# A batch-norm matmul: row-wise spread by small copies, one block turned behind the last product, one fused scale and shift

## The chip, the cores and the metric

The kernel runs on one core of a Trainium2 chip. The metric is the device time of one execution in microseconds (us); the time shown for a kernel is the median of its runs. Five engines work side by side, each in the order of its own queue: PE (TensorE, matrix products), DVE (VectorE), ACT (ScalarE), POOL (GpSimd) and SP (SyncE, which here only issues transfers). Transfers are carried out by 16 DMA engines that all queues share.

## The reference

```python
def reference(x, weight, gamma, beta, eps):      # x: 16 x 512 x 1024, weight: 1024 x 768
    y = np.matmul(x, weight)
    mean = np.mean(y, axis=(0, 1), keepdims=True)
    var = np.var(y, axis=(0, 1), keepdims=True)
    y_norm = (y - mean) / np.sqrt(var + eps)
    return (gamma * y_norm + beta).astype(np.float32)
```

x has 8192 rows of 1024 numbers, the output 8192 rows of 768 channels, all float32. Every channel is normalized over all 8192 rows, so that no output of a channel can be written before all of that channel's products are done.

## The kernel before

**Tiling.** The rows are cut into 16 chunks c of 512, the channels into 6 tiles nt of 128, counted from 0. x is loaded as bf16 and transposed by DVE into `xT_sb`. All of x and all products stay in the core's memory, the products as bf16 in `y_sb`.

**Tiles 0 and 1** are computed with the rows on the partitions. Their mean and square sums pass through `sum1`, `sum2` and `sum3`, which are free afterwards. When the statistics are known, `spread` (L894, a float32 product with the identity `ident32`) lays scale and shift out along a row in a PSUM bank, DVE multiplies (L930), POOL or DVE adds (L935), and SP stores.

**Tiles 2 to 5** are computed with the channels on the partitions, one unit `col_unit` of 8 products of 128x512 per chunk (L568). DVE takes statistics (L704), ACT copies the products out of PSUM (L708). `finish_tasks` combines the statistics into scale and shift. Then blocks of two chunks (1024 rows) are normalized in place (L1016 on ACT for tile 2, L1019 on DVE for tiles 3 and 4) and must be turned back, since the output has the rows outermost. `col_block` does it in one of two ways, by `MODE`:
- "xact": SP issues a DMA transpose (L1190), ACT converts the result to float32 (L1202), SP stores (L1172).
- "pe": PE makes 8 transposes of 128x128 (L1037) into a PSUM bank, ACT copies the bank to float32 (L1180), SP stores. The transposes are hosted: `mm` puts one of them behind each product of a later unit.

**Raw blocks.** The blocks at chunks 0 and 2 of tiles 2 and 4 are turned by a DMA transpose before they are normalized (L1099), at about 100 us. Their scale and shift then lie along the row as for tiles 0 and 1: `raw_spread` (L1119) makes two float32 products into a bank (L896), and ACT copies the shift half to `sum2` (L1130). `raw_block` multiplies on DVE out of the bank (L1144), adds on POOL out of `sum2` (L1148) and stores (L1152).

**Copies of x.** `xT_sb` of most chunks interleaves pairs of contraction rows, so that a product reads it with a stride of two. For the chunks in `PARTED` ACT makes a contiguous copy `x_pl` early on; for those in `LATE`, `part_chunk` has POOL or DVE make it (four copies of 128x1024 for a chunk, L540) for the units of tiles 4 and 5. The chunks in `SINGLE` are transposed without the interleave.

**The end.** The last chunk of tile 5 is multiplied in two halves (`last_unit`, L746). Then, one after the other: DVE's statistics of the last half (L753), `aggregate` (L1254), `root` on ACT (L1257), `affine` on DVE (L1264 to L1266), the first `norm_part` (L1289), PE's transposes (L1037), ACT's copy (L1302) and SP's store (L1305), for 11 pieces of 256 to 1024 rows.

**What sets the order.** Each step is a `task` with a due time, its engines, its dependences and a cost written by hand. `arrange` (L122) plays these through once and emits the instructions of every engine in the order that results; a list of 8 PSUM banks, slots of the ring buffer for outgoing blocks and the like take part. At run time each queue is in order: an instruction that waits holds up all behind it.

Of the kernel before, what the change touches and what calls it, by code (L numbers as in the profile page):

```python
# [227 lines left out]
def kernel(  # L228
# [9 lines left out]
    nc = tc.nc  # L238
# [28 lines left out]
    GY = 2  # L267
    PAD = 54
    HELD = 0
    ASTAT = {2:tuple(range(4,16))}  # L270
    RC = C - 2
    XT, YB, SQ = C - EARLY, 28, 3
    ADDED = (0,6,16,28,40)
    PARTED, LATE, SINGLE = (4,5,7,8,9,10), (12,13,14,15,11), (2,3,6)
    MODE = {2:'xact',3:'xact',4:('pe',)*2+('xact',)*1+('pe',)*5}
    MODE = {nt: m if isinstance(m, tuple) else (m,) * (C // GY) for nt, m in MODE.items()}
# [62 lines left out]
    rstd = singles.tile([P, 1], f32)  # L339
    warm = singles.tile([P, 1], f32)  # L340

    seq(nc.scalar.activation(warm, eps_sb, AF.Sqrt))
# [9 lines left out]
    def task(prio, engines, emit, deps=(), lock=False, **kw):  # L352
        t = Task(prio, engines, emit, deps, **kw)
        t.lock = lock
        tasks.append(t)
        return t
# [10 lines left out]
    def pe(occ):  # L367
        return {"PE": (occ, occ + 0.03)}
# [72 lines left out]
    for kind, n, *n1 in order:  # L441
# [12 lines left out]
        if m0 == M // 2:  # L454
            affine = task(t, {"SP": (5.0, 7.0)}, load_affine, [x_ready[m0 // CH - 3, 0, JW]])
        slot = Slot(rings, rows // 32 * KQ // 2)
# [662 lines left out]
    def raw_spread(nt, fin_task):  # L1119
        bank = Slot(banks)  # L1120
        at = (0, NA, 2 * NA)[nt - GA] // 2

        def emit(eng):
            a_ps = psum.tile([P, CH], f32, tag="b")
            bank.tile = a_ps
            spread(a_ps[:, 0:P], scale, nt)
            spread(a_ps[:, P:2 * P], shift, nt)

        def keep(eng):
            seq(nc.scalar.copy(sum2[:, at:at + P], bank.tile[:, P:2 * P]))  # L1130

        t = task(clock[0] + 1.0, pe(0.45), emit, [fin_task], takes=[bank])
        k = task(clock[0] + 1.0, act(0.25), keep, [t], uses=[bank])
        raw_aff[nt] = bank, t, k, sum2[:, at:at + P]

# [25 lines left out]
    def col_block(nt, c, due, fin_task, held=False):  # L1161
# [46 lines left out]
        return b  # L1208

    held = []  # L1210
    STEP = {2: 1.9, 3: 2.3, 4: 2.3}
# [47 lines left out]
    def first_term(eng):  # L1259
        seq(nc.vector.scalar_tensor_tensor(  # L1260
            tmp[:, one], mv[:, nt, 0:1], -1.0, gamma_sb[:, one], op0=ALU.mult, op1=ALU.mult))

    def affine(eng):
        seq(nc.vector.reciprocal(rstd, std[:, one]))  # L1264
        seq(nc.vector.tensor_mul(scale[:, one], rstd, gamma_sb[:, one]))
        seq(nc.vector.scalar_tensor_tensor(  # L1266
            shift[:, one], tmp[:, one], rstd, beta_sb[:, one], op0=ALU.mult, op1=ALU.add))

# [4 lines left out]
    ft = task(E - 50.0, dve(0.1), first_term, [ag])  # L1273
    af = task(E - 50.0, dve(0.45), affine, [ro, ft])
    for i, (hn, hc, hf) in enumerate(held):
        b = col_block(hn, hc, E + 0.3 + 0.3 * i, hf)
        b.deps.append(col_end[nt, C - 1, len(PIECES) - 1][0])
    ends = [(0, 0, QR), (0, QR, QR), (1, 0, CH), (2, 0, CH)] + [(c, 0, 2 * CH) for c in range(3, C - 1, 2)]
    ends += [(C - 1, 0, CH)]
    for c, r0, rows in ends:  # L1280
# [5 lines left out]
        for i in range(n):  # L1286
            def norm_part(eng, c=c + i, r0=r0, rows=min(rows, CH)):
                part = y(nt, c)[:, r0:r0 + rows]
                seq(nc.vector.tensor_scalar(  # L1289
                    part, part, scale[:, one], shift[:, one], op0=ALU.mult, op1=ALU.add))  # L1290

            norms.append(task(due + 0.6 * i, dve(0.323 if rows >= CH else 0.26), norm_part, [af] + keeps,
                              uses=[y_of(nt, c + i)]))
# [59 lines left out]
```

## Time and profile before

| what | value |
|---|---|
| median of 3 runs | 207.62 us (207.26 to 207.69) |
| profiled execution, device time | 207.92 us |
| its span, first to last instruction | 206.0 us |
| mean granted clock of TensorE in the span | 0.981 |
| busy: PE, DVE, ACT, POOL | 191.4, 157.6, 139.5, 129.4 us |
| read from and written to memory | 36.71 MB and 25.17 MB |
| DMA transposes L1190, L1099 | 15 and 4 |

The profiled execution took 207.92 us, of which 1.92 us lie around its span; it is 0.30 us above the median of the runs. Up to about 100 us the kernel loads x and multiplies tiles 0 and 1, and parts of the others, as x comes in; from there to 188.4 us PE multiplies tiles 2 to 5 while the outputs of the earlier tiles are normalized, turned and stored. From 188.4 us tile 5's statistics are closed and its 4.2 MB are normalized, turned and stored. A busy time counts an instruction from its start to its end, also where the next one overlaps it; the granted clock is the share of TensorE's full clock that its throttle gave it, and the DMA share is the mean over the 16 DMA engines.

### The profile page before, as it was taken

The page shows a single profiled execution, that of the slowest core. Times are in us where ns is not written, and L with a number is a line of the kernel's source. Part 1 is how long each engine was busy: PE and PEld are TensorE (multiplying, and loading weights), DVE is VectorE, ACT ScalarE, POOL GpSimd, SP SyncE. Part 2 cuts the span into 40 slices and gives each one's busy share as a digit, 9 for nine tenths or more (in the row PEclk, how much of TensorE's full clock was granted, in tenths as well). Part 3 has the DMA queues.
Part 4 walks back from the last instruction along what each step waited for, and adds up shares of the span by engine and source line. Part 5 has one row for each costly group of instructions (what it writes and reads, how often), then busy time and mean ns, then how long its engine had stood idle before and what let it go on. Part 6 is the DMA issues. An engine that isn't in the chain of part 4 may idle for free.

```text
span 206.0 us, 3500 instructions
## 1 busy us (share of the span) xinstructions
PE 191.4 (93%) x1218; PEld 117.8 (57%) x1218; DVE 157.6 (76%) x239; ACT 139.5 (68%) x248; POOL 129.4 (63%) x143
## 2 busy tenths in 40 slices
PE   7979999999999999999999999999999999996910
PEld 3457564747488888777875444444444445553900
DVE  4022879999999999969989998888999648947900
ACT  2000561369979999998979767996575877875960
POOL 7676964887499989997304998599955440440000
PEclk9999999999999999999999999999999999999695
DMA  4999999999999999999665898899999999999898
GB/s 76 143 199 196 174 196 196 196 198 196 190 193 197 197 196 197 196 197 195 109 153 179 311 339 300 253 349 278 294 325 233 322 312 296 338 344 346 250 347 254
DMA packets 98561, 48.73 MB, mean 237 GB/s; under 512 B 24304, under 2 KB 98032, under 8 KB 98544
## 3 DMA queue, kind: packets, MB, share of 16 engines
q0 software_dynamic: 34624, 18.36, 64.9%
q1 hardware_dynamic: 63920, 30.16, 52.9%
q8 instruction: 9, 0.15, 0.3%
q14 instruction: 8, 0.07, 0.1%
HBM read 36.71 MB, written 25.17 MB: 300 GB/s over the span
## 4 chain that ended last, share of the span: by engine, by line
PE 86%; DMA 3%; ACT 3%; POOL 3%; issue 1%; DVE 1%; ACTq 0%; POOLq 0%
PE y_ps L568 53%; PE y_ps L503 24%; PE y_ps L807 4%; DMA ring<-in_x_dram 3%; ACT o_sb L1302 3%; PE o_ps L1037 2%; POOL ring L399 1%; POOL w_sb L383 1%; PE a_ps L896 1%; PE y_ps L746 1%; PE o_ps L1067 0%; ACTq L1348 0%; PE idle_ps L584 0%; PE tot_ps L864 0%; DVE fin L753 0%
## 5 line engine op out<-in xcount | busy, mean ns | idle before, releaser
L568 PEld LDWEIGHTS <-w_sb 128*128 128x128 bf16 x520 | 50.4, 97 | 56.9
L568 PE MATMUL y_ps<-x_pl,w_sb 128*128 128x512 bf16 x264 | 61.3, 379 | 0.0
L399 POOL DMA_DIRECT2D ring<-in_x_dram x76 | 47.4, 630 | 14.0 <-DMA ring<-in_x_dram 5.4
L568 PE MATMUL y_ps<-xT_sb,w_sb 128*128 128x512 bf16 (+1 forms) x256 | 55.7, 370 | 0.0
L503 PE MATMUL y_ps<-w_sb,xT_sb 128*128 128x256 bf16 x448 | 50.4, 272 | 1.3 <-DMA ring<-in_x_dram 1.2
L503 PEld LDWEIGHTS <-xT_sb 128*128 128x128 bf16 x448 | 43.7, 98 | 8.6 <-DVE xT_sb L428 1.9
L428 DVE STREAM_TRANSPOSE xT_sb<-ring 128x1024 f32<-128x1024 f32 (+1 forms) x29 | 31.2, 1111 | 14.4 <-DMA ring<-in_x_dram 14.3
L704 DVE BATCH_NORM_STATS2 stats<-y_ps 128x6 f32<-128x512 f32 x46 | 30.6, 686 | 11.2 <-PE y_ps L568 11.0
L708 ACT CAST y_sb<-y_ps 128x512 bf16<-128x512 f32 x51 | 29.2, 591 | 13.8 <-DVE stats L704 11.6
L935 POOL TENSOR_TENSOR ring<-ring,sum 128x1024 f32<-128x1024 f32 (+1 forms) x11 | 23.8, 2186 | 14.6 <-ACT y_ps L717 11.1
L652 ACT ACTIVATE sq_sb<-y_ps 128x512 f32<-128x512 f32 x28 | 16.4, 611 | 18.6 <-PE y_ps L503 18.3
L659 POOL TENSOR_TENSOR sum<-sum,sq_sb 128x512 f32<-128x512 f32 x20 | 25.6, 1280 | 3.8 <-ACT sq_sb L652 2.7
L540 ACT COPY x_pl<-xT_sb 128x1024 bf16<-128x1024 bf16 x24 | 24.4, 1054 | 1.7 <-DVE xT_sb L428 1.7
L655 DVE TENSOR_TENSOR sum<-y_ps,sum 128x512 f32<-128x512 f32 x28 | 18.9, 675 | 6.4 <-ACT sq_sb L652 5.3
L665 ACT CAST y_sb<-y_ps 128x512 bf16<-128x512 f32 x28 | 16.0, 601 | 7.7 <-DVE sum L655 7.4
L540 POOL COPY x_pl<-xT_sb 128x1024 bf16<-128x1024 bf16 x15 | 16.4, 1131 | 7.7 <-DVE x_pl L540 4.9
L1202 ACT CAST ring<-ring 128x1024 f32<-128x1024 bf16 x15 | 15.8, 1050 | 2.5 <-DMA ring<-y_sb 2.3
L930 DVE TENSOR_TENSOR ring<-y_sb,a_ps 128x1024 f32<-128x1024 bf16 (+1 forms) x16 | 16.7, 1079 | 0.7 <-DMA out_dram<-ring 0.7
L1148 POOL TENSOR_TENSOR ring<-ring,sum 128x1024 f32<-128x1024 f32 x4 | 9.7, 2422 | 10.9 <-DVE ring L1144 10.8
L1037 PE MATMUL o_ps<-ident,y_sb 128*128 128x128 bf16 x104 | 14.5, 248 | 2.1 <-DVE y_sb L1289 2.0
L421 DVE STREAM_TRANSPOSE xT_sb<-ring 128x2048 bf16<-128x2048 bf16 x6 | 13.5, 2288 | 0.2 <-DMA ring<-in_x_dram 0.2
L584 PE MATMUL idle_ps<-idle_sb 128*128 128x512 f32 x18 | 10.9, 765 | 1.5 <-DVE idle_sb L315 1.5
(97 smaller groups left out, 154.8 us busy)
## 6 DMA issues: line engine op xcount, KB each, us to landing
out_dram<-ring SPq DMA_DIRECT2D x38, 512.0 KB, 3.8
ring<-in_x_dram POOLq DMA_DIRECT2D x52, 256.0 KB, 8.7
out_dram<-o_sb SPq DMA_DIRECT2D x6, 512.0 KB, 4.4
ring<-in_x_dram POOLq DMA_DIRECT2D x16, 128.0 KB, 6.2
w_sb<-in_weight_dram POOLq DMA_DIRECT2D x8, 192.0 KB, 6.2
out_dram<-ring SPq DMA_DIRECT2D x4, 256.0 KB, 3.1
ring<-in_x_dram POOLq DMA_DIRECT2D x4, 192.0 KB, 7.9
out_dram<-o_sb SPq DMA_DIRECT2D x3, 256.0 KB, 2.5
```

Of the source, the lines that this page charges most:

```text
L399: bi = seq(nc.gpsimd.dma_start(x_bf[32 * i:32 * i + 32], src[:, :, KQ * i:KQ * (i + 1)]))
L428: seq(nc.vector.transpose(dst, src[:, :, jw0:jw1]))
L503: seq(nc.tensor.matmul(y_ps[:, s], x_of(c, jw, e, t * P, (t + 1) * P), w_sb[:, jw, e, 0:NA], start=(s == 0 and jw == 0 and e == 0), stop=( ...
L540: seq(nc.scalar.copy(dst, pairs) if eng == "ACT" else ENG[eng].tensor_copy(dst, pairs))
L568: seq(nc.tensor.matmul(y_ps, w_sb[:, jw, e, nt * P:(nt + 1) * P], moving(c, jw, e, q0 * QR, q1 * QR, parted), start=(jw == 0 and e == 0 an ...
L655: seq(nc.vector.tensor_add(sum1, slot.tile[:, 0:n], sum1))
L659: seq(ENG[eng].tensor_add(acc, acc, state["sq"][:, 0:n]))
L704: seq(nc.vector.bn_stats(dst, slot.tile))
L708: seq(nc.scalar.copy(y(nt, c), slot.tile))
L930: seq(nc.vector.tensor_mul(slot.o, y_row[c].y[:, s0:s1], aff[0][:, None, :].to_broadcast([P, n, NA])))
L935: seq(ENG[eng].tensor_add(slot.o, slot.o, row[:, None, :].to_broadcast([P, n, NA])))
L1037: seq(nc.tensor.transpose(dst, src, ident))
```

## The change

The diff does the following:
- `raw_spread` uses no products any more. DVE copies the scale column and the shift column into two 32-wide fields of `sum1` and transposes them in 32x32 blocks into `sum3` (`turn`). Four copies of 32x2x32 gather the four partition groups into a row on the first 32 partitions of `sum2` (`gather`), and three copies of 32x256 deal this row to the other partition groups (`deal`). Gather and deal may each run on POOL or ACT; in the emitted order both stand on POOL for tile 2, and for tile 4 gather stands on ACT and deal on POOL. ACT then copies the row of 256 into a PSUM bank (`keep`). POOL's add reads the shift half in `sum2` as before, DVE's multiplication the scale half in the bank.
- Chunk 11 leaves `LATE`: its `x_pl` is not made, and the units of tiles 4 and 5 read it from `xT_sb`. Chunk 10, its neighbour, leaves the group of late chunks too, which moves both in the order of tile 3.
- `MODE[4]` is "pe" for all blocks. Before, its third entry (chunks 4 and 5) was "xact"; the first two entries belong to the raw blocks.
- `HELD` is 1: the block of chunks 14 and 15 of tile 4 is given to the new function `held_block`. It is normalized early, its 8 transposes stand on PE behind the last product (two groups of 4 in two banks), ACT copies each group (128x512), and SP stores each (256 KB). The second copy and the copy-out of the very last products (`last_keep`, L756) stand behind `root` on ACT.
- The last scale and shift come from one instruction over two columns: `coef` holds gamma and minus mean times gamma, `base` holds 0 and beta, and `fss = coef * rstd + base`. The constant columns are filled on POOL (`terms`, three small instructions, in its queue behind the merging of the sums at L793).
- `PAD`, the unused columns behind the statistics, goes from 54 to 50; three two-column tensors (`coef`, `base`, `fss`) are new.

In the emitted order of the changed kernel the four float32 products per raw tile are gone from PE, 40 hosted transposes of tile 4 remain (five blocks, as before), the last of them one unit earlier, and 8 stand between the last product and tile 5's own transposes.

```diff
--- before.py
+++ after.py
@@ -265,14 +265,14 @@
     GA = 2
     NA = GA * P
     GY = 2
-    PAD = 54
-    HELD = 0
+    PAD = 50
+    HELD = 1
     ASTAT = {2:tuple(range(4,16))}
     RC = C - 2
     XT, YB, SQ = C - EARLY, 28, 3
     ADDED = (0,6,16,28,40)
-    PARTED, LATE, SINGLE = (4,5,7,8,9,10), (12,13,14,15,11), (2,3,6)
-    MODE = {2:'xact',3:'xact',4:('pe',)*2+('xact',)*1+('pe',)*5}
+    PARTED, LATE, SINGLE = (4,5,7,8,9,10), (12,13,14,15), (2,3,6)
+    MODE = {2:'xact',3:'xact',4:('pe',)*8}
     MODE = {nt: m if isinstance(m, tuple) else (m,) * (C // GY) for nt, m in MODE.items()}
     RAW, RAWADD, RAWDUE = {2:(0,2),4:(0,2)}, {2:'POOL',3:'POOL',4:'POOL'}, {2:14.0,3:8.0,4:8.0}
     RING = 3 * CH // 32 * KQ // 2
@@ -338,6 +338,9 @@
     tmp = singles.tile([P, NT], f32)
     rstd = singles.tile([P, 1], f32)
     warm = singles.tile([P, 1], f32)
+    coef = singles.tile([P, 2], f32)
+    base = singles.tile([P, 2], f32)
+    fss = singles.tile([P, 2], f32)
 
     seq(nc.scalar.activation(warm, eps_sb, AF.Sqrt))
     touched = singles.tile([P, 2, TOUCH], f32)
@@ -452,7 +455,7 @@
         rows = n1[0] if kind == "p" else QR if kind == "x" else CH
         m0 = n if kind == "p" else n * rows
         if m0 == M // 2:
-            affine = task(t, {"SP": (5.0, 7.0)}, load_affine, [x_ready[m0 // CH - 3, 0, JW]])
+            affine_loads = affine = task(t, {"SP": (5.0, 7.0)}, load_affine, [x_ready[m0 // CH - 3, 0, JW]])
         slot = Slot(rings, rows // 32 * KQ // 2)
         between = BETWEEN if m0 == 0 else {}
         also = sum(len(v) for v in between.values())
@@ -1118,20 +1121,41 @@
 
     def raw_spread(nt, fin_task):
         bank = Slot(banks)
-        at = (0, NA, 2 * NA)[nt - GA] // 2
-
-        def emit(eng):
+        k = sorted(RAW).index(nt)
+        row = sum2[:, 2 * P * k:2 * P * (k + 1)].rearrange("p (i n) -> p i n", n=P)
+        wide, turned = sum1[:, NA + 64 * k:NA + 64 * (k + 1)], sum3[:, 64 * k:64 * (k + 1)]
+        both = turned.rearrange("p (i n) -> p i n", n=32)
+        now = clock[0] + RAWDUE[nt] + 2.0
+
+        def quadrant(i):
+            return slice(32 * i, 32 * i + 32)
+
+        def turn(eng):
+            for i, src in enumerate((scale, shift)):
+                seq(nc.vector.tensor_copy(wide[:, quadrant(i)], src[:, nt:nt + 1].to_broadcast([P, 32])))
+            seq(nc.vector.transpose(turned, wide))
+
+        def move(eng, dst, src):
+            seq(nc.scalar.copy(dst, src) if eng == "ACT" else nc.gpsimd.tensor_copy(dst, src))
+
+        def gather(eng):
+            for i in range(4):
+                move(eng, row[0:32, :, quadrant(i)], both[quadrant(i)])
+
+        def deal(eng):
+            for i in range(1, 4):
+                move(eng, row[quadrant(i)], row[0:32])
+
+        def keep(eng):
             a_ps = psum.tile([P, CH], f32, tag="b")
             bank.tile = a_ps
-            spread(a_ps[:, 0:P], scale, nt)
-            spread(a_ps[:, P:2 * P], shift, nt)
-
-        def keep(eng):
-            seq(nc.scalar.copy(sum2[:, at:at + P], bank.tile[:, P:2 * P]))
-
-        t = task(clock[0] + 1.0, pe(0.45), emit, [fin_task], takes=[bank])
-        k = task(clock[0] + 1.0, act(0.25), keep, [t], uses=[bank])
-        raw_aff[nt] = bank, t, k, sum2[:, at:at + P]
+            seq(nc.scalar.copy(a_ps[:, 0:2 * P], row.rearrange("p i n -> p (i n)")))
+
+        d = task(now, dve(0.35), turn, [fin_task], True)
+        g = task(now, {"POOL": (0.8, 0.85), "ACT": (0.9, 1.0)}, gather, [d])
+        s = task(now, {"POOL": (1.2, 1.25), "ACT": (1.0, 1.1)}, deal, [g])
+        t = task(now, act(0.4), keep, [s], takes=[bank])
+        raw_aff[nt] = bank, t, s, row[:, 1]
 
     def raw_block(nt, c, due):
         rslot, turned = raw[nt, c]
@@ -1206,6 +1230,27 @@
             task(due + 1.2, {"SP": (0.38, 0.4)}, store, [d], dma=count * P * P * 4 / 1024 * STORE * 1.024,
                  uses=[slot])
         return b
+
+    def held_block(nt, c, due, fin_task, last_mm, root_task):
+        yslot = y_of(nt, c)
+        keeps = [col_end[nt, c + i][1] for i in range(GY)]
+        count = RT
+        a = task(due - 20.0, dve(0.45), norm(nt, c, GY), [fin_task] + keeps, True, uses=[yslot])
+        for i in range(GY):
+            slot = Slot(rings, count * P)
+            m0 = (c + i) * CH
+            b, bank = turn_block(due - 1.0 + 0.1 * i, nt, m0, count, [a, last_mm], [yslot])
+
+            def copy(eng, slot=slot, bank=bank):
+                slot.o = piece(slot).rearrange("p (s n) -> p s n", n=P)
+                seq(nc.scalar.copy(slot.o, bank.tile))
+
+            def store(eng, slot=slot, m0=m0):
+                seq(nc.sync.dma_start(
+                    out_flat[m0:m0 + count * P, nt * P:(nt + 1) * P].rearrange("(s p) n -> p s n", p=P), slot.o))
+
+            d = task(due - 60.0 + 15.0 * i, act(0.48), copy, [b] + ([root_task] if i else []), takes=[slot], uses=[bank])
+            task(due, {"SP": (0.38, 0.4)}, store, [d], dma=count * P * P * 4 / 1024 * STORE * 1.024, uses=[slot])
 
     held = []
     STEP = {2: 1.9, 3: 2.3, 4: 2.3}
@@ -1258,23 +1303,28 @@
 
     def first_term(eng):
         seq(nc.vector.scalar_tensor_tensor(
-            tmp[:, one], mv[:, nt, 0:1], -1.0, gamma_sb[:, one], op0=ALU.mult, op1=ALU.mult))
+            coef[:, 1:2], mv[:, nt, 0:1], -1.0, gamma_sb[:, one], op0=ALU.mult, op1=ALU.mult))
+
+    def terms(eng):
+        seq(nc.gpsimd.tensor_copy(coef[:, 0:1], gamma_sb[:, one]))
+        seq(nc.gpsimd.memset(base[:, 0:1], 0.0))
+        seq(nc.gpsimd.tensor_copy(base[:, 1:2], beta_sb[:, one]))
 
     def affine(eng):
         seq(nc.vector.reciprocal(rstd, std[:, one]))
-        seq(nc.vector.tensor_mul(scale[:, one], rstd, gamma_sb[:, one]))
-        seq(nc.vector.scalar_tensor_tensor(
-            shift[:, one], tmp[:, one], rstd, beta_sb[:, one], op0=ALU.mult, op1=ALU.add))
+        seq(nc.vector.scalar_tensor_tensor(fss, coef, rstd, base, op0=ALU.mult, op1=ALU.add))
 
     su = task(E - 5.0, dve(0.5), sum_up, [col_end[nt, c][0] for c in range(C - 2)])
     ag = task(E - 50.0, dve(0.25), aggregate,
               [su, col_end[nt, C - 2][0]] + [col_end[nt, C - 1, q][0] for q in range(len(PIECES))])
     ro = task(E - 50.0, {"ACT": (0.2, 0.3)}, root, [ag])
     ft = task(E - 50.0, dve(0.1), first_term, [ag])
-    af = task(E - 50.0, dve(0.45), affine, [ro, ft])
-    for i, (hn, hc, hf) in enumerate(held):
-        b = col_block(hn, hc, E + 0.3 + 0.3 * i, hf)
-        b.deps.append(col_end[nt, C - 1, len(PIECES) - 1][0])
+    te = task(E - 30.0, pool(0.3), terms, [affine_loads, sr])
+    af = task(E - 50.0, dve(0.35), affine, [ro, ft, te])
+    last_bn, last_keep = col_end[nt, C - 1, len(PIECES) - 1]
+    for hn, hc, hf in held:
+        held_block(hn, hc, E, hf, last_bn.deps[0], ro)
+        last_keep.deps.append(ro)
     ends = [(0, 0, QR), (0, QR, QR), (1, 0, CH), (2, 0, CH)] + [(c, 0, 2 * CH) for c in range(3, C - 1, 2)]
     ends += [(C - 1, 0, CH)]
     for c, r0, rows in ends:
@@ -1287,7 +1337,7 @@
             def norm_part(eng, c=c + i, r0=r0, rows=min(rows, CH)):
                 part = y(nt, c)[:, r0:r0 + rows]
                 seq(nc.vector.tensor_scalar(
-                    part, part, scale[:, one], shift[:, one], op0=ALU.mult, op1=ALU.add))
+                    part, part, fss[:, 0:1], fss[:, 1:2], op0=ALU.mult, op1=ALU.add))
 
             norms.append(task(due + 0.6 * i, dve(0.323 if rows >= CH else 0.26), norm_part, [af] + keeps,
                               uses=[y_of(nt, c + i)]))
```

## The prediction

> **What bounds the kernel now.** I read the chain of waits first, then its pieces at the end, then the busy table by stretches, then single groups. The chain of the page says who ended last:
>
> ```profile
> PE 86%; DMA 3%; ACT 3%; POOL 3%; issue 1%; DVE 1%; ACTq 0%; POOLq 0%
> ```
>
> PE carries the chain, and in its list of pieces (start us, length us, what) no wait lies between 100 and 188.4 us: everything there is products in a row, so a product taken off PE moves all that follows.
>
> ```profile
> 127.97 0.44 PE a_ps L896 x4
> ...
> 172.68 0.44 PE a_ps L896 x4
> ...
> 184.85 1.73 PE y_ps L568 x8
> 186.58 1.83 PE y_ps L746 x16
> 188.41 0.02 issue
> 188.43 0.44 DVE fin L753
> 188.87 0.02 issue
> 188.90 0.37 ACT y_sb L756
> 189.27 0.21 ACT std L1257
> 189.48 0.03 issue
> 189.51 0.17 DVE rstd L1264
> 189.68 0.02 issue
> 189.71 0.16 DVE scale L1265
> 189.86 0.14 DVE shift L1266
> 190.01 0.03 issue
> 190.03 0.35 DVE y_sb L1289
> ```
>
> Two things are to be seen: each raw tile's spread costs PE 0.44 us, and from the last product (188.41) to tile 5's first normalization (190.03) the steps follow one another for 1.62 us. The busy table by stretches (columns: stretch, its length, busy us of PE, PEld, DVE, ACT, POOL, granted clock, DMA share, GB/s) shows the second resource:
>
> ```profile
> 184.00:188.40 4.40, 4.39 (x31) 2.59 (x28) 2.52 (x6) 3.69 (x6) 0.00 (x0) 1.00 1.15 347
> 188.40:190.80 2.40, 0.37 (x4) 0.23 (x4) 2.06 (x9) 0.62 (x3) 0.00 (x0) 1.00 1.15 345
> 190.80:193.20 2.40, 2.36 (x24) 2.09 (x23) 2.40 (x9) 2.09 (x5) 0.00 (x0) 0.62 0.54 160
> 193.20:196.00 2.80, 2.80 (x40) 2.80 (x38) 2.28 (x8) 2.80 (x4) 0.00 (x0) 0.72 1.09 329
> 196.00:204.60 8.60, 0.26 (x5) 0.08 (x2) 0.00 (x0) 2.92 (x4) 0.00 (x0) 0.83 1.15 347
> ```
>
> The DMA engines run at 345 to 347 GB/s both before and after a hole at 190.8 to 193.2, where they move 160. Tile 4's backlog is sent by about 191.0; tile 5's first store is issued at 191.15, and its data moves from about 192.0, so an issue takes some 0.9 us to show. The hole and the ramp to 196 cost (347-160)/347 x 2.40 + (347-329)/347 x 2.80 = 1.29 + 0.15 = 1.44 us. Behind it, tile 5's 4194 KB need 12.1 us at 347 GB/s. So the end is "first store of tile 5, plus ramp, plus 12.1 us", and what starts tile 5 earlier ends the kernel earlier, until the hole is full.
>
> **The change, part by part.** The sum is made on the profiled execution, 207.92 us (span 206.0), 0.30 above the median of 207.62.
>
> *Products of the spread removed.* 2 x 0.44 = 0.88 us off PE, all of it on the path.
>
> *Chunk 11 not copied.* Two units (tiles 4 and 5) become strided. In PE's timeline five strided units start at 113.43 and end where the next, contiguous one starts, at 122.47: 9.04 / 5 = 1.81 us; a contiguous unit is 1.73. So +0.16 us on PE. Off the path, four copies of chunk 11 disappear; POOL made four at 163.31 to 167.31, the last of all copies, and tile 4's last unit stood behind them, spread out between tile 5's products. Tile 4 can only close earlier.
>
> *Tile 4 by TensorE alone, one block held.* Five hosted blocks before and after, 40 transposes; the eight of chunks 4 and 5 come in, the eight of chunks 14 and 15 go behind the last product. Net 0 on the path before 188.4. One DMA transpose goes: in the stretch of transposes SP's pairs (transpose and store) repeat every 2.6 us (164.32, 166.99), a store of 512 KB alone takes 524 / 347 = 1.5, so it frees about 1.1 us of the DMA engines (bounds: 0.9 by its 262 KB of the 786 KB moved in a pair, to the 1.93 that its issue occupies SP). This is hidden by the backlog and only makes the hole open sooner.
>
> PE therefore ends at 188.41 - 0.88 + 0.16 = 187.69.
>
> *The held block in the hole.* Its transposes follow the last product on an idle PE (8 x 0.055 = 0.44 us within the 2.04 us that PE waits there). Backlog without it ends at 191.0 - 1.1 - 1.5 = 188.4; its first copy is done near 188.6, issue and 0.9 us put its data at 189.6, and 1.5 us of data end at 191.1. Tile 5's first data is due at 192.05 less the gain below, 191.25. They just fit, so the held block pushes nothing back. If its copy is over 0.15 us later than I say, each further 0.1 us costs at most as much.
>
> *The chain at the end.* ACT now has held copy 1 ahead of the root. It starts some 0.33 us after the transposes (as ACT's first copy did behind PE at 190.43), and a copy of this shape takes 0.61 us (the three 128x512 copies of L1302), so root can end 1.15 us behind the last product instead of 1.07: +0.08, bounds -0.12 (the 0.12 us for which L756 held up the root is gone, should the copy be early) and +0.6 (the whole copy). The fused step replaces 0.16 + 0.14 by one instruction not shown at this width; its one-column form L1266 takes 0.21 against the 0.30 of the pair with its handover: -0.12, bounds -0.2 and 0. Sum -0.04; what is late next would be the root alone.
>
> *The ramp.* The granted clock falls to 0.5 at about 191.3, after PE waited 2.04 us, and PE needs 1.80 us for 16 transposes, so that the first 1024-row copy starts at 192.84. At full clock the four small copies before it (till 192.57) would be the limit: 0.27 us. With the held transposes the gap shrinks to about 1.2 us. I take -0.1, bounds -0.27 and 0.
>
> By the Trainium skill, "TensorE: Matmul & The Clock Gate", Part 1, the clock falls only after an idle window of some 3.4 us, and by its Part 4 transposes do not count as busy. By that the held transposes do nothing and this term is 0; but this trace lost its clock after 2.04 us without work and regained it during transposes alone, so here I go by the rows.
>
> *Small copies in other queues.* Not shown at their size. POOL gets seven in tile 2 and three in tile 4: at least 0.23 us each (the 128x128 memset of the identity), at most 1.13 (a 128x1024 copy, L540); nearest is a two-input add of 128x256, L793, 0.76, so for one input I take 0.4: 2.8 and 1.2 us, bounds 1.6 to 7.9 and 0.7 to 3.4. DVE's turn: twice three instructions between 0.12 (L873) and 0.68 (L428 at 128x512), together at most 2 us per tile. ACT gets a 256-wide copy, 0.37 (L908), and for tile 4 four gathers at 0.19 to 0.26, and loses the two copies L1130 (0.26). The three `terms` run on POOL at 105 to 111 us, where it waits 11.1 us for ACT. All this lies off PE: the cover is that DVE sits idle 8.2 us between 165 and 190 waiting for PE, ACT waited 3.40 us before 150.68, and POOL had gaps of 1.63 and 3.29 us before 151.39 and 156.87. Queued behind them are POOL's copies of chunks 12 to 15 and, on ACT behind the copy into the bank, the copies that free PE's banks. Cost taken 0, and a gain is excluded since nothing on the path waits for them.
>
> A rule speaks against this part. "SBUF — State Buffer", section "SBUF: two separate sides", says that DVE and POOL take a shared pair of ports as an exclusive lock, the loser blocking for the whole instruction. The trace agrees: beside POOL's three copies from 146.75, tile 3's two tiny scale and shift steps took 0.87 and 1.05 us, against 0.16 and 0.21 in tile 4. By the rule each of the ten POOL copies may hold a DVE step for its length, 4 us by my price; I keep 0, since PE did not wait there either.
>
> *Sum.* -0.88 + 0.16 - 0.04 - 0.1 = -0.86 us: 207.06 for the profiled execution, 206.76 for the median.
>
> **The rivals.**
> - *The root waits for the held block* (14%). For: the copy stands before root on ACT and needs PE's transposes and a ring slot; ACT's first copy behind PE is the slowest handover of the tail. Against: the slot it takes belongs to a store several places earlier in the backlog. With the upper bounds, +0.6 and no ramp gain, no fused gain: -0.72 + 0.6 = -0.12, 207.5. This is no change.
> - *POOL's queue turns into the bound* (16%). Place: tile 4's unit of chunk 15, whose four copies must come from POOL and DVE. In the new order its first products stand 36 products before the first hosted transpose (171.5), so they are due near 163.7; POOL ended that chunk's copies at 160.57. So from 3.1 us of lateness PE waits, us for us. Seven small copies at 0.76 make 5.3 us; if the gaps (waits for DVE) move along with the queue and absorb nothing, PE stalls 2.2 us: 207.62 - 0.86 + 2.2 = 209.0, slower. Against: at 0.4 the lateness is 2.8, below the point, and one chunk's copies are gone.
> - *The hole closes better than I count* (12%). Full clock, the copy early, the fused step at its best: -0.72 - 0.12 - 0.2 - 0.27 = -1.31, 206.3. The total of DMA work allows 1.44 + 1.1, so it doesn't forbid it.
> - That the change does not do what it says is excluded for PE by the emitted order, where the four products are gone.
>
> **How the numbers follow.** Forecast 58%: 206.76, its own range 206.4 to 207.2. Faster by over 0.2% (about 0.42 us, about what a measurement of this kernel can tell from no change) are nearly all of the forecast (0.57), the better hole (0.12) and little of the first rival (0.01): 0.70. Slower: the queue, 0.16. Same: the rest, 0.14. The range goes down to the better hole with a little noise, 206.1, and up past the first rival towards the queue at a small excess (a stall of 1.1 us), 207.9.
>
> **What would show it.** Right: no L896 from 110 us on; the last product at 187.6 to 187.8; root's end about 1.15 us behind it; first normalization near 189.3; the stretch behind the backlog moving over 250 GB/s instead of 160; last DMA byte near 203.8. Wrong: PE waiting for POOL or ACT at L568 between 140 and 172, or for y_sb at a hosted transpose (tile 4's first norm done after 171.5); a root more than 1.4 us behind the last product; tile 5's first store later than 190.6.

## The result, and the profile after

| | before | changed |
|---|---|---|
| median of runs, us | 207.38 (207.0 to 207.69, 6 runs) | 206.32 (205.87 to 206.54, 6 runs) |
| ratio to before, 95% interval | | 0.9951 (0.9936 to 0.9965) |
| profiled execution, its span | 207.92, 206.0 | 206.43, 204.6 |

The change gains 1.06 us; 0.86 was forecast. Of the 1.4 us between the two spans, 0.61 come up while x is still loading and are put down to chance: the chain passes the stage's first product (L807, after the change L810) at 97.48 us before and at 96.87 after, and the other executions below have it anywhere between 96.5 and 97.3, whatever the kernel. So all positions below that are called "from the anchor" are counted from that product of the same execution. Line numbers of the changed kernel are 3 higher up to `raw_spread`, 24 to 50 higher behind it; in the kernel before with the new `raw_spread` alone they are 21 higher behind it.

The page's chain, shares by engine, of the changed kernel:

```profile
PE 79%; DMA 9%; ACT 3%; POOL 2%; issue 1%; DVE 1%; ACTq 0%; DVEq 0%; POOLq 0%
```

PE's share is 7 points lower and DMA's 6 higher than before only because the chain takes another way through the loading at the start; from the anchor to the last product it is PE alone again. The end of the chain of waits of the changed kernel (start us, length us, what):

```profile
185.24 1.81 PE y_ps L749 x16
187.05 0.24 PE o_ps L1040 x4
187.29 0.03 ACTq L1246
187.32 0.04 issue
187.36 0.58 ACT ring L1246
187.94 0.20 ACT std L1302
188.15 0.02 issue
188.17 0.17 DVE rstd L1314
188.34 0.02 issue
188.37 0.23 DVE fss L1315
188.60 0.03 issue
188.62 0.36 DVE y_sb L1339
188.98 0.05 issue
189.03 0.54 PE o_ps L1040 x4
```

The last product ends at 187.05, 90.18 from the anchor (before: 188.41, 90.93): 0.75 us less. Root ends 1.10 us behind it (before 1.07), the first normalization starts 0.47 behind root (before 0.55). The held block's first copy (L1246) now stands on the chain, but DVE's aggregate, which root needs as well, ends at 187.81, and root ends 0.34 us behind that, as before (0.33): the copy holds up nothing.

The busy table by stretches of the changed kernel (stretch, its length, busy us of PE, PEld, DVE, ACT, POOL, granted clock, DMA share, GB/s):

```profile
184.00:188.00 4.00, 3.50 (x30) 2.45 (x28) 2.92 (x9) 2.19 (x5) 0.00 (x0) 1.00 1.15 346
188.00:189.00 1.00, 0.00 (x0) 0.00 (x0) 0.76 (x5) 0.88 (x3) 0.00 (x0) 1.00 0.37 108
189.00:190.40 1.40, 1.33 (x15) 0.83 (x16) 1.40 (x5) 1.01 (x3) 0.00 (x0) 1.00 1.14 343
190.40:192.00 1.60, 1.60 (x23) 1.11 (x22) 1.60 (x6) 1.60 (x4) 0.00 (x0) 1.00 0.78 234
192.00:196.00 4.00, 2.52 (x32) 1.66 (x30) 2.07 (x7) 4.00 (x6) 0.00 (x0) 1.00 1.15 346
196.00:203.20 7.20, 0.00 (x0) 0.00 (x0) 0.00 (x0) 1.10 (x2) 0.00 (x0) 0.71 1.14 343
```

The hole of 2.4 us at 160 GB/s has become two dips: 1.0 us at 108 GB/s between tile 4's backlog (its stores that still wait for the DMA engines) and the held block, and 1.6 us at 234 while tile 5 starts. The granted clock stays 1.00 through both. The last byte moves 106.5 us from the anchor; before it was 107.3.

### The profile page after: what moved, and what is told of

Read it like the earlier page. It is cut to its first block, busy times and chain, and to the rows that moved or that the text cites. A ratio compares the mean times of both kernels' runs of the same rounds, so it can differ in the third digit from the quotient of the medians.

```text
span 204.6 us, 3497 instructions
## 1 busy us (share of the span) xinstructions
PE 188.8 (92%) x1203; PEld 115.1 (56%) x1218; DVE 158.5 (77%) x243; ACT 140.3 (69%) x253; POOL 129.5 (63%) x153
## 4 chain that ended last, share of the span: by engine, by line
PE 79%; DMA 9%; ACT 3%; POOL 2%; issue 1%; DVE 1%; ACTq 0%; DVEq 0%; POOLq 0%
PE y_ps L571 50%; PE y_ps L506 21%; DMA w_sb<-in_weight_dram 6%; PE y_ps L810 4%; ACT o_sb L1352 3%; DMA ring<-in_x_dram 3%; PE o_ps L1040 2%; POOL ring L402 1%; PE y_ps L749 1%; POOL w_sb L386 1%; DVE xT_sb L431 1%; PE a_ps L899 1%; PE o_ps L1070 0%; ACTq L1398 0%; PE tot_ps L867 0%
## 5 line engine op out<-in xcount | busy, mean ns | idle before, releaser
L571 PE MATMUL y_ps<-xT_sb,w_sb 128*128 128x512 bf16 (+1 forms) x264 | 58.7, 371 | 0.4
L571 PE MATMUL y_ps<-x_pl,w_sb 128*128 128x512 bf16 x241 | 56.7, 379 | 0.4
L707 DVE BATCH_NORM_STATS2 stats<-y_ps 128x6 f32<-128x512 f32 x46 | 30.8, 686 | 10.1 <-PE y_ps L571 9.8
L655 ACT ACTIVATE sq_sb<-y_ps 128x512 f32<-128x512 f32 x28 | 16.5, 613 | 17.1 <-PE y_ps L506 16.4
L1226 ACT CAST ring<-ring 128x1024 f32<-128x1024 bf16 x14 | 14.7, 1049 | 1.8 <-DMA ring<-y_sb 1.8
L543 POOL COPY x_pl<-xT_sb 128x1024 bf16<-128x1024 bf16 x12 | 13.3, 1139 | 2.1 <-DVE x_pl L543 2.0
L1139 POOL COPY sum<-sum 32x256 f32<-32x256 f32 (+1 forms) x10 | 3.4, 344 | 12.4 <-ACT sum L1139 11.6
L587 PE MATMUL idle_ps<-idle_sb 128*128 128x512 f32 x18 | 9.6, 685 | 1.5 <-DVE idle_sb L315 1.5
```

What stands on the lines that cost most here:

```text
L543: seq(nc.scalar.copy(dst, pairs) if eng == "ACT" else ENG[eng].tensor_copy(dst, pairs))
L571: seq(nc.tensor.matmul(y_ps, w_sb[:, jw, e, nt * P:(nt + 1) * P], moving(c, jw, e, q0 * QR, q1 * QR, parted), start=(jw == 0 and e == 0 an ...
L707: seq(nc.vector.bn_stats(dst, slot.tile))
```

## The experiments

The same columns for all runs. "Closed": tile 4's scale and shift are ready. "Last byte": the end of the last packet of the stores. All in us from the anchor, except the medians. The medians of before in these runs were 207.16 to 207.49, so the ratios are the safer comparison.

| run | median | ratio (95% interval) | last product | closed | last byte |
|---|---|---|---|---|---|
| before | | 1 | 90.9 | 74.1 | 107.3 |
| changed, again | 206.14 | 0.9939 (0.9919 to 0.9960) | 90.2 | 72.0 | 106.5 |
| spread_on_pe | 207.20 | 0.9997 (0.9981 to 1.0014) | 91.1 | 69.7 | 107.3 |
| held_off | 206.93 | 0.9980 (0.9964 to 0.9996) | 90.7 | 72.0 | 106.8 |
| xact_back | 207.44 | 1.0003 (0.9988 to 1.0018) | 89.8 | 72.0 | 107.4 |
| t3_block_by_pe | 206.20 | 0.9955 (0.9938 to 0.9971) | 90.3 | 72.3 | 106.5 |
| copy_11 | 207.79 | 1.0031 (1.0019 to 1.0043) | 90.0 | 76.9 | 108.1 |
| spread_alone | 208.73 | 1.0075 (1.0056 to 1.0094) | 90.0 | 76.9 | 109.0 |
| spread_no_11 | 206.74 | 0.9970 (0.9953 to 0.9988) | 90.2 | 72.0 | 107.0 |
| t3_affine_act | 206.22 | 0.9942 (0.9923 to 0.9961) | 90.2 | 71.8 | 106.4 |
| t3_affine_act_xact | 207.49 | 1.0006 (0.9992 to 1.0021) | 89.7 | 71.8 | 107.3 |
| slow_spread | 215.65 | 1.0410 (1.0385 to 1.0434) | 99.0 | 77.4 | 115.7 |
| t3_all_pe | 213.45 (one execution) | | 95.6 | 74.7 | 113.7 |

The parts don't add up: going back on any one of four (spread, held block, chunks 4 and 5, chunk 11) costs 0.8 to 1.7 us by the medians, and all together brought 1.1 to 1.3. The ledger below explains most of it. It takes 0.2-us stretches from 64 us behind the anchor to the last byte, counts what each lacks to 346 GB/s as idle DMA time, and the rest as work; work plus idle is the whole stretch.

| us | work | idle 64 to 74 | idle 74 to 84 | idle 84 to 100 | idle from 100 |
|---|---|---|---|---|---|
| before | 39.9 | 1.3 | 0.4 | 1.5 | 0.3 |
| changed | 39.2 | 0.7 | 1.0 | 1.3 | 0.4 |
| spread_on_pe | 38.9 | 0.8 | 1.0 | 2.6 | 0.2 |
| held_off | 39.2 | 0.7 | 0.5 | 2.3 | 0.2 |
| xact_back | 40.1 | 0.7 | 1.1 | 0.1 | 1.4 |
| t3_block_by_pe | 39.4 | 0.7 | 0.6 | 1.7 | 0.2 |
| copy_11 | 39.3 | 1.5 | 1.6 | 0.2 | 1.6 |
| spread_alone | 40.0 | 1.6 | 1.7 | 0.1 | 1.6 |
| spread_no_11 | 40.5 | 0.7 | 0.4 | 0.7 | 0.7 |
| t3_affine_act | 38.8 | 0.8 | 1.1 | 1.5 | 0.2 |
| t3_affine_act_xact | 39.6 | 0.8 | 1.4 | 0.2 | 1.4 |

Two regimes are to be seen. Where PE is late, idle time stands between 84 and 100 (the hole and the start of tile 5), and PE's last product sets the end. Where it is 0.1 to 0.2 there, the DMA engines never run dry, and it makes no difference how early PE ends. The time from the last product to the last byte says the same: 16.2 to 16.4 us in the seven executions with 1.3 us or more idle between 84 and 100 (before, changed twice, spread_on_pe, held_off, t3_block_by_pe, t3_affine_act), 16.8 in spread_no_11, and 17.5 to 19.0 in xact_back, copy_11, spread_alone and t3_affine_act_xact.

**The kernel as changed, once more**, as a measure for its neighbours.

> The changed kernel once more, as the measure for the others on this chip: 206.3, ratio to before 0.993 to 0.997. If the 0.6 us by which its profile was ahead at the first product of the stage at L807/L810 came from the loading's own scatter, this profile's distance from that product to the last is again 90.2, whatever the start does.

206.14 us, the last product 90.18 from the anchor, as in the first profile.

**The spread by products, all else as changed.**

```diff
 def raw_spread(nt, fin_task):    # as before: two float32 products into a bank, ACT copies the shift half
```

> The changed kernel with the raw blocks' spread made by products again (two float32 products per raw tile, the shift half copied by ACT); all else as changed. Theory (the path is PE's products, so what is taken off PE comes out of the time): from the first product of the stage at L807/L810 to the last product 90.18 + 0.88 = 91.06 us, the time 0.88 us above the changed kernel, some 207.2. Rival (DMA work or the end decides and PE has slack): the last product 0.88 later, but the last DMA byte less than 0.4 later, time 206.3 to 206.7.

207.20 us, 1.06 more than the changed kernel beside it; the last product is 0.94 later, the last byte 0.8, and the ledger puts it all into the hole (2.6 for 1.3), which is back behind the last product (188.03):

```profile
188.00:189.60 1.60, 0.48 (x9) 0.31 (x6) 1.22 (x5) 1.27 (x5) 0.00 (x0) 1.00 0.06 17
```

PE sets the end here, and the spread's products cost what they take.

**No held block.**

```diff
-    HELD = 1
+    HELD = 0
```

> The changed kernel with HELD = 0: the block of chunks 14 and 15 of tile 4 is turned by hosted transposes like the others. Theory: 8 more transposes of 0.055 us ahead of the last product, so the last product 0.44 later (90.62 from the stage's first product), the root about 0.05 to 0.1 earlier behind it, net +0.35 to +0.45, some 206.7; the hole in the DMA between tile 4 and tile 5 widens by 1.5 us less what moves. The clock falls to 0.5 behind the last product again, and if the ramp cost I priced at 0.1 is real the tail is 0.1 longer. Rival (the held block only fills the hole and the DMA decides): as fast as the changed kernel.

206.93: 0.79 more by the medians, 0.47 and 0.53 in the profiled executions (206.96 for 206.49 and 206.43). The last product is 0.47 later, the last byte 0.3. The rest of the 0.79 shows in no trace; the two ratios' intervals allow anything from 0.1 to 1.6 us. The clock had been expected to fall behind the last product again; it stayed 1.00 until 198.89.

**Chunks 4 and 5 of tile 4 by a DMA transpose again; then one block of tile 3 by PE as well.**

```diff
-    MODE = {2:'xact',3:'xact',4:('pe',)*8}
+    MODE = {2:'xact',3:'xact',4:('pe',)*2+('xact',)*1+('pe',)*5}                         # xact_back
+    MODE = {2:'xact',3:('xact',)*7+('pe',)*1,4:('pe',)*2+('xact',)*1+('pe',)*5}          # t3_block_by_pe
```

> The changed kernel with the block of chunks 4 and 5 of tile 4 turned by a DMA transpose again, the rest of tile 4 as changed. Theory (PE first, DMA close behind it): 8 transposes less on PE, last product 0.44 earlier (89.74 from the stage's first product), but 1.1 us more DMA work, so tile 4's backlog and the held block end at about the time tile 5's first data is due or 0.4 later: the time falls by 0 to 0.4, 205.9 to 206.3. Rival A (PE alone decides): 0.44 faster, 205.9. Rival B (DMA work decides): slower by up to 0.7, 207.0.

> xact_back once more, with the last block of tile 3 turned by TensorE instead: as many DMA transposes (14 and 4) and as many transposes on PE as the changed kernel, at another place. DMA theory (the number of DMA transposes decides whether a hole is left in which the slow DMA engines catch up): as the changed kernel, last product 90.2 from the stage's first product, a hole of over 0.5 us behind tile 4, some 206.2. Rival (it is the place in tile 4 that costs, where SP has the transpose ahead of tile 4's first stores): as xact_back, some 207.4.

PE's last product came 0.43 us earlier, and the kernel was 1.3 us slower, more than even the rival of DMA work allowed. The stretches at the end of xact_back's profile show it (columns as above):

```profile
202.60:202.80 0.20, 0.00 (x0) 0.00 (x0) 0.00 (x0) 0.00 (x0) 0.00 (x0) 0.50 0.98 287
202.80:203.20 0.40, 0.00 (x0) 0.00 (x0) 0.00 (x0) 0.00 (x0) 0.00 (x0) 0.50 0.21 63
203.20:203.60 0.40, 0.00 (x0) 0.00 (x0) 0.00 (x0) 0.00 (x0) 0.00 (x0) 0.50 0.14 41
203.60:204.00 0.40, 0.00 (x0) 0.00 (x0) 0.00 (x0) 0.00 (x0) 0.00 (x0) 0.50 0.07 22
204.00:204.40 0.40, 0.00 (x0) 0.00 (x0) 0.00 (x0) 0.00 (x0) 0.00 (x0) 0.50 0.05 14
```

A sixteenth of 347 GB/s is 21.7. So, by this estimate, at 202.8 three of the 16 engines have work left, then two, then one, which ends 1.6 us behind the others. In the changed kernel the same trickle fills its first dip (46 and 44 GB/s from 188.2 to 188.6). I read it so: there the slow engines catch up while the others wait for tile 5; without a dip the trickle stands at the end and is paid. With one block of tile 3 moved to PE instead, the dip is back (1.0 us), and so is the time: 206.20. One DMA transpose costs the same in either tile, which is what the theory of DMA work expected.

**Chunk 11 copied again; the spread alone; the spread without chunk 11.** The first is the changed kernel, the other two are the kernel before with the new `raw_spread`.

```diff
-    ..., (12,13,14,15), (2,3,6)
+    ..., (12,13,14,15,11), (2,3,6)         # copy_11, spread_alone; spread_no_11 is without 11
```

> The changed kernel with the copies of chunk 11 back: two units contiguous again, four copies more in POOL's and DVE's queues. PE theory: last product 0.16 earlier (90.02 from the stage's first product), 206.0, if POOL's queue is not late for the last chunk. Rival 1 (POOL's queue): the last copies are late, PE waits at L571 and the last product is 0.3 to 2 later. Rival 2 (DMA): the last product 0.16 earlier but the time the same, as the hole shrinks below what the slow DMA engines need.

> The kernel before with one part of the change alone, the raw blocks' spread by small copies instead of products. PE theory (as in the prediction): last product 0.88 earlier, and all of it comes out of the time, some 206.3 beside 207.16. DMA theory (formed from xact_back, where one to three of the 16 DMA engines went on for 1.6 us after the others): in the kernel before the last of those engines finishes tile 4 at 192.0, just as tile 5's first data comes, so with tile 5 0.88 earlier the slowest engine never catches up; the last product is 0.88 earlier, but the last DMA byte at most 0.5, with a trickle of 20 to 60 GB/s at its end, some 206.7 or more.

> The kernel before with two parts of the change only: the spread without products, and chunk 11 not copied. Theory (the two belong together): with the spread's ten copies in POOL's queue, the four copies of chunk 11 close tile 4 late, 76.9 us after the stage's first product, and the DMA engines starve before tile 5; without them tile 4 closes near 72 us, PE's last product stands at 90.2 (90.04 + 0.15), and the end is that of the run that went back to the DMA transpose, which has the same number of them: 207.2 to 207.6, against 208.7 for the spread alone. Rival 1 (chunk 11's copies matter little, the spread alone is slow by its own copies and by the DMA transpose): 208.4 to 208.9. Rival 2 (PE decides, so that the spread's 0.88 is kept and only the held block's part is missing): 206.5 to 206.8.

The spread alone takes PE's 0.88 us away (90.93 to 90.04) and makes the kernel 1.5 us slower. Dropping chunk 11's copies adds 0.16 on PE and makes it 2.0 faster than that (2.2 by the ratios). Undone in the changed kernel, chunk 11's part costs 1.65. None of the expectations for copy_11 and spread_alone had such sizes; the DMA theory for spread_alone had the direction alone. The stretches of 5 us of copy_11, from 79 us behind its anchor:

```profile
175.53:180.53 5.00, 5.00 (x39) 2.81 (x37) 4.06 (x7) 5.00 (x8) 2.83 (x7) 1.00 0.84 252
180.53:185.53 5.00, 5.00 (x33) 2.80 (x32) 4.00 (x8) 3.32 (x6) 4.68 (x2) 1.00 1.15 343
```

and of the changed kernel at the same place:

```profile
175.87:180.87 5.00, 5.00 (x38) 2.78 (x38) 3.15 (x5) 4.93 (x8) 4.72 (x2) 1.00 1.15 343
180.87:185.87 5.00, 4.95 (x30) 2.63 (x29) 2.68 (x6) 2.37 (x4) 0.00 (x0) 1.00 1.15 346
```

At 252 GB/s, 1.4 us of DMA time is lost while tile 4's blocks are not ready, since tile 4 closes 4.9 us later (76.9 for 72.0); the ledger has the same 1.4 us more idle time between 64 and 84 (3.1 for 1.7). The wait list of SP in spread_alone from 160 to 190 us (engine, line waited for: us in total, times, longest us) begins with

```profile
SPq L1211 <- DVE y_sb L1019: 5.4, 3, 2.2
```

where the changed kernel has 1.3 us at the same step. Why does tile 4 close late? My expectation for spread_no_11 blamed POOL's queue at run time. That fell: POOL ends chunk 11's four copies 69.5 us from the anchor in spread_alone, and at 69.8 in the kernel before. What moved is the order that `arrange` writes. PE's products of L568 from the anchor to tile 4's aggregate, the first step of its closing, in spread_alone and then in spread_no_11 (stretch, length, busy us of PE and PEld with counts, clock, DMA share, GB/s; a few matmul records are missing, so the weight loads, PEld, count better):

```profile
96.52:171.18 74.66, 65.08 (x297) 28.81 (x298) 1.00 0.97 266
```

```profile
96.84:167.25 70.41, 60.32 (x271) 26.88 (x278) 1.00 0.96 264
```

Before has 286 weight loads up to there. Tile 4's last unit thus stands about 12 products later in the written order once the spread is made by copies, and some 20 products (4.3 us at 0.217) earlier without chunk 11. The aggregate began 2.15 us later and 4.25 earlier, tile 4 closed 2.8 later and 4.9 earlier; the 0.7 between is `root` in spread_alone, which ACT starts only 0.85 us behind the aggregate. Without chunk 11 the spread's copies move the aggregate by the same 2.15 us (spread_on_pe to changed, 68.28 to 70.43). That POOL's planned time is what shifts it fits, but was not tried by itself.

For spread_no_11 itself 206.74 is the number of its second rival, not of my theory (207.2 to 207.6, "the end of xact_back"). It has the same DMA transposes as xact_back, and its PE ends 0.4 later, yet it is 0.7 faster. In the ledger it has 0.7 us less idle between 74 and 84 and 0.7 less at the end, against 0.6 more between 84 and 100 and 0.4 more work; its last byte is 0.4 earlier. The first is in the 1-us stretches, xact_back and then spread_no_11:

```profile
176.00:177.00 1.00, 0.95 (x10) 0.53 (x9) 0.78 (x1) 0.97 (x2) 0.08 (x1) 1.00 0.34 101
```

```profile
176.00:177.00 1.00, 1.00 (x9) 0.62 (x8) 0.96 (x1) 1.00 (x3) 0.00 (x0) 1.00 1.15 347
```

The order differs on DVE. From 72.06 us in xact_back it makes two of tile 4's normalizations ahead of a statistics step (L707), from 72.05 in spread_no_11 one (L704), so that the step ends 0.48 us later. ACT's copy-out, tile 4's four gather copies and the next conversion of tile 3 (at 75.64 for 75.16) wait for it in a row. So part of xact_back's loss is this idle time and not the transpose's own work; the changed kernel has the order and the idle time too (1.0), but there the hole hides it. The trickle at the end of xact_back is longer as well (1.6 us against 0.6), which stays unexplained.

**POOL's small copies four times as long.**

```diff
         def move(eng, dst, src):
-            seq(nc.scalar.copy(dst, src) if eng == "ACT" else nc.gpsimd.tensor_copy(dst, src))
+            for _ in range(1 if eng == "ACT" else 4):
+                seq(nc.scalar.copy(dst, src) if eng == "ACT" else nc.gpsimd.tensor_copy(dst, src))
```

> The changed kernel with each of the ten small copies on POOL made four times (to the same place): 3 x 2.35 = 7.05 us more in POOL's queue in tile 2 and 3 x 1.44 = 4.3 us in tile 4, the order of all instructions as before. Step of the prediction: POOL's copies for chunk 15, ready at 160.98 in the changed kernel and due at about 163.1 to 166, come 5.0 (both gaps of 1.31 and 0.71 absorb) to 7.05 us later, so PE waits 0 to 2 us at L571 and the last product is later by as much, 206.2 to 208.2. Rival (POOL is off the path at any such price): no wait of PE, 206.2.

PE's waits in this run (columns as for SP's):

```profile
PE y_ps L571 <- DVE x_pl L543: 3.1, 3, 2.1
PE o_ps L1040 <- ACT y_sb L711: 2.6, 1, 2.6
...
PE y_ps L571 <- ACT y_sb L711: 0.6, 1, 0.6
```

Tile 2's seven copies took 9.9 us instead of 2.35, POOL ended chunk 15's copies at 168.1 instead of 160.98, and PE waited 6.3 us for what stood behind; its clock also fell to 0.5 for 3.41 us from 184.53. The last product came 8.9 us later, where 0 to 2 had been expected, and the kernel was 9.5 us slower (215.65 for 206.14), with 11.8 us more of small copies on POOL. The prediction's rival of POOL's queue has its mechanism right, though the loss was larger than it counts. It did not decide because the real prices are low. All instructions of L1139 in the changed kernel (count: ns min/median/max, first and last start, forms):

```profile
L1139 POOL COPY sum<-sum x10: 227/388/569, 136.3 to 173.6; 32x256 f32<-32x256 f32 x6, 32x64 f32<-32x64 f32 x4
L1139 ACT COPY sum<-sum x4: 242/243/243, 171.5 to 172.2; 32x64 f32<-32x64 f32 x4
```

**Tile 3 wholly by PE.**

```diff
-    MODE = {2:'xact',3:'xact',4:('pe',)*8}
+    MODE = {2:'xact',3:'pe',4:('pe',)*8}
```

> Tile 3's eight DMA transposes are replaced by 64 transposes on PE; everything else as in the changed kernel. PE's last product must come 64 x 0.055 = 3.5 us later (93.7 us after the stage's first product, against 90.18), so the time rises to about 209.7 under both theories. They differ in what the DMA engines do behind tile 4's backlog. If the DMA transposes make a few of the 16 engines lag, the stretch in which only one to three engines still move data (20 to 60 GB/s) shrinks from 1 us in the changed kernel (188.0 to 189.0) to under 0.5 us. If the lag comes from the stores or the loads, it stays at about 1 us.

A single execution, 213.45 us where 209.7 had been expected, the last product 95.6 from the anchor, 1.9 later than by the 64 transposes (1.5 us are PE's waits for normalized blocks). Its DMA engines in the two places asked for, behind tile 4's backlog and then twice in tile 5:

```profile
190.00:190.40 0.40, 0.40 (x4) 0.19 (x2) 0.18 (x2) 0.08 (x1) 0.00 (x0) 1.00 1.14 347
190.40:190.80 0.40, 0.40 (x6) 0.34 (x4) 0.31 (x1) 0.00 (x0) 0.00 (x0) 1.00 0.21 55
190.80:193.60 2.80, 1.91 (x21) 1.53 (x19) 1.85 (x7) 1.99 (x5) 0.00 (x0) 1.00 0.00 0
...
197.80:198.80 1.00, 1.00 (x12) 1.00 (x11) 1.00 (x4) 1.00 (x2) 0.00 (x0) 0.50 0.08 14
...
209.60:210.40 0.80, 0.00 (x0) 0.00 (x0) 0.00 (x0) 0.00 (x0) 0.00 (x0) 0.50 0.06 19
```

Behind the backlog the trickle is 0.4 us, as the theory that DMA transposes cause it expected. But one engine lags by 0.8 to 1.0 us twice in tile 5, where there are only stores and all engines had been empty for 2.8 us. So the transposes are not the only cause of the trickle, and what else causes it stays open.

**Tile 3's scale and shift on ACT; the same with chunks 4 and 5 by DMA transpose.**

```diff
-        if nt > GA:
+        if nt > GA + 1:
```

> Tile 3's scale and shift go to ACT instead of DVE, so that the two tiny steps that took 0.87 and 1.05 us beside POOL's copies of x no longer hold up tile 3's first normalization. Theory that the DMA engines' work is a resource in balance with PE: SP starts tile 3's transposes about 1.2 us earlier, the hole between tile 4's backlog and tile 5's data opens about that much earlier, PE's last product stays at 90.2 us after the stage's first, and the time stays within 0.3 us of the changed kernel's 206.2, since PE sets the start of tile 5 there. Rival (DMA work still decides the end of the changed kernel): faster by 0.5 to 1.2 us, 205.0 to 205.7.

> As the run with tile 3's scale and shift on ACT, and chunks 4 and 5 of tile 4 are turned by a DMA transpose again. PE's last product comes 0.44 us earlier than in the changed kernel (89.75 us after the stage's first). If the theory of balance is right, the DMA work now ends about 1.2 us earlier than in the run that only went back to the DMA transpose (207.4), so that a part of PE's gain is kept: 205.7 to 206.3. Rival: the last DMA engines still end 1 to 2 us behind the others and the end stays at 207.0 to 207.5, whatever tile 3 does.

206.22 and 207.49: no gain with either. SP issued tile 3's first transpose earlier (53.1 us from the anchor instead of 54.2), but its last at 71.9, as in the changed kernel (71.8): in between it waited for DVE's statistics (6.8 us in all, 5.5 in the changed kernel). The DMA time won at the start of tile 3 was not kept (0.2 us more idle between 64 and 84, 0.2 more in the hole), and the expectation that the hole opens earlier fell, with the second run's hope of a version better than both. No version tried was faster than the changed kernel beyond the intervals.

## Why the prediction was right, and where not

- *Spread off PE, -0.88.* Right: 0.94 on PE, 1.06 in time when undone in the changed kernel. What the prediction did not see is the condition: done alone, the same 0.88 came with a loss of 1.5 us, through the emitted order.
- *Chunk 11, +0.16.* PE's part was right (0.15). "Tile 4 can only close earlier" was right as well (74.1 to 72.0 from the anchor), but it was given no value, as off the path, and this step failed: the four copies cost 1.65 us in the changed kernel and 2.0 with the spread alone. A late tile 4 starves the DMA engines some 10 us before the hole, and that fills the hole from the other side.
- *One DMA transpose less frees 1.1 us, "hidden by the backlog and only makes the hole open sooner".* The size was good (0.9 us of work in the ledger of xact_back), the "hidden" was wrong: with the transpose back, the DMA engines have no dip left behind tile 4, their work sets the end, and PE's gain is lost. Undone it costs 1.3 us, part of which is the idle time behind DVE's order.
- *PE ends 0.72 us earlier.* Measured 0.75.
- *The held block fits the hole.* Right: its data follows the first dip, and the first store of tile 5 is issued 2.70 us behind the last product (before 2.74). Of the prediction's signs one was just missed: behind the backlog, from 188.0 to 190.4, 245 GB/s moved and not over 250. The rival in which root waits for it fell: root's end came 1.10 behind the last product, between before's 1.07 and the 1.15 expected.
- *The chain, -0.04.* +0.03 at root and -0.08 by the fused step.
- *The ramp, -0.1.* The size was near, the reason was luck. With the clock at 1.00 the first 1024-row copy of tile 5 starts 3.96 us behind the last product (held_off the same), and 4.43 in the kernel before, whose clock falls 2.95 us behind that product. In spread_no_11 it falls 3.42 behind, and the copy starts at 4.21. With the early copy the dip that followed before is gone. The stretch that begins 5.99 us behind the last product, in the kernel before and then in the changed one:

```profile
194.40:195.20 0.80, 0.80 (x13) 0.80 (x12) 0.80 (x4) 0.80 (x2) 0.00 (x0) 0.77 0.96 289
193.04:193.84 0.80, 0.80 (x13) 0.51 (x11) 0.80 (x4) 0.80 (x2) 0.00 (x0) 1.00 1.15 346
```

  From 3.6 to 7.2 us behind the last product, the kernel before lacks 0.52 us of DMA time and the changed one 0.34. But the last byte comes only 0.05 nearer to the last product (16.31 for 16.36): the changed kernel ends in a trickle (142 GB/s in its last 0.4 us, before 248). The first 1.6 us of the ramp do not hang on the clock; spread_no_11 moves 226 GB/s there at half clock, the changed kernel 234:

```profile
190.40:192.00 1.60, 1.60 (x18) 1.50 (x17) 1.60 (x6) 1.49 (x3) 0.00 (x0) 0.52 0.76 226
```

  Nor does the clock stay up by virtue of the held transposes, as the prediction had it: held_off has none and keeps it, spread_on_pe has them and loses it at 192.17.
- *Small copies, 0.* Their price of 0.4 was near (0.23 and 0.42), and PE waited for none of them. Their cost was not in any wait but in the plan.

In the sum, the last byte stands 0.80 us nearer to the anchor, close to the forecast's 0.86; 0.86 also lies within the interval of the ratio (0.9959). It came out by luck: the two largest terms that it left at nothing have opposite signs, what the spread's copies do to the order (+1.5 us alone, where -0.9 was due, so +2.4) and what dropping chunk 11 takes away again (-2.2 by the ratios, where +0.16 was due). By ratios the spread and chunk 11 together bring 0.30% (0.6 us), the other three parts 0.2 to 0.3% (0.4 to 0.6).

## What to carry to other kernels

Where a transfer queue and an engine are both nearly full at the end, keep a ledger of the queue's work and idle time beside the chain of waits: the chain showed PE alone, and still chunk 11's copies and the DMA transpose worked through the DMA engines, and the spread's gain depended on them. An edit "off the path" is worth nothing only if it does not change when a tile closes; with a planner, look at where the tile's last unit stands in the emitted order, not only at waits. Undo the parts one by one and also do one alone: here four of them were worth 0.8 to 1.7 us each in company, and the spread alone cost 1.5.

## What the runs showed of the hardware

- The 16 DMA engines do not finish together: by the rates above, one to three lag 0.4 to 1.6 us behind, in stretches with and without DMA transposes. The Trainium skill, "DMA: Bandwidth & Descriptors", section "Latency and other measured facts", says that engines 7 and 15 are usually slower and gives a guess as the cause; the profile here shows only how many lag, not which.
- The clock's fall does not follow the length of PE's pause. In held_off it stayed 1.00 behind a pause of 1.97 us, in spread_on_pe it fell at 192.2 behind one of 1.53, in the changed kernel the same 1.53 us left it up until 198.97. The Trainium skill, "TensorE: Matmul & The Clock Gate", Part 1, has the activity window run freely, so that the phase decides. These three fit that in part. The granted clock falls and rises again after 3.41 us (191.36 to 194.77 in the kernel before), and counted in such steps 1.26 us of spread_on_pe's pause lie in the step that ends with the fall (188.76 to 192.17), the rest of which holds transposes alone. In the changed kernel 1.24 us of the pause lie in the step up to 188.74, which holds products ahead of it, and 0.29 in the next. So the place of the pause among the other work mattered here; how much transposes count, these traces do not settle.
- Two one-column steps on DVE took 0.87 and 1.05 us beside POOL's copies of x (tile 3), 0.16 and 0.21 without (tile 4), while the one-input step between, the reciprocal, took 0.15 and 0.16; moving them to ACT made tile 3's first normalization 1.3 us earlier, without any gain in time.
